# Two layers of a hybrid diffusion backbone: the RWKV branch's preparation and state copy on VectorE instead of GpSimd

## The chip, the core and the metric

The kernel is one program on one core of a Trainium2 chip. The metric is the device time of an execution in microseconds (us). The core has five instruction streams that the profile shows: PE (TensorE's matrix products; PEld is the loading of the stationary operand that runs beside them), DVE (VectorE), ACT (ScalarE), POOL (GpSimd) and SP (SyncE, which here only issues transfers). Each runs its own instructions in a fixed order and waits on semaphores for the others.

## The reference, cut to what matters

One inference step of a two-layer backbone over 384 tokens (128 context, 256 latent) with model width 1024. A layer is a gated feed-forward half step, a mixer, and a second feed-forward half step. The mixer sums three gated branches: windowed attention, neighbourhood attention, and a bidirectional RWKV-7 recurrence with 8 heads of 64 channels, in both directions `d`. Only this last branch is touched:

```
kk = normalised(k * k_k)                        # per head
for d in (forward, backward):
    decay = exp(-exp(-softplus(-(w0[d] + tanh(wlo) @ decay_up[d])) - 0.5))
    a     = sigmoid(a0[d] + alo @ iclr_up[d])
    k_d   = k * (1 + (a - 1) * k_a)
    S     = start state
    for t in tokens of d:
        sa = S @ (-kk_t)
        S  = S * decay_t + outer(sa, kk_t * a_t) + outer(v_t, k_d_t)
        y_t += S @ r_t
    bonus += sum(r * k_d * r_k, per head) * v
out = (group_norm(y) + bonus) * g
```

## The kernel before

**Dense work.** Every large product is 128x128 weights against 128x384 activations, done in three passes with operands split into a high and a low part (`hi`, `lo`); L400 to L402 are the three passes in the mixer. Weights stream from memory in units of eight blocks as `raw`; ACT makes `hi<-raw`, and DVE makes `lo<-raw,hi`.

**The recurrence.** It is computed in chunks of 64 tokens. The eight heads go in four pairs `p` = 0 to 3 (two heads fill 128 partitions), and each pair goes through three generators:

- `rwkv_prepare` makes, for each direction, the running decays `wq` and `wi` (a scan on DVE after an exponential on ACT), the key `kd`, and from them two operands of the chunk algebra: `bk` (half of it `ta` times `wq`, the other half `kd` times `wq`) and `arc` (`r` times `wi` in one half, `nkk` times `wi` in the other). At its end `bo` sums the two directions' `kd` and multiplies by `r` for the bonus; the product `bon` spreads it.
- `rwkv_chunks` transposes `bk` (`pb`), forms the chunks' Gram products (`pg`, masked into `gt` by DVE), inverts a 64x64 triangular system per chunk (block transposes `lu`, short products and reductions in `pr` and `gt`, transposes `yr` and `xt`, four groups of small products called `pz`), and forms `mt`, `rp`, `nt`, `yt`.
- `rwkv_scan` carries the state from chunk to chunk (`sp`, `scan`, `state`), then normalises (`gm`, `gss`) and gates.

**What orders it.** `rwkv_gen` interleaves them: while the chunks of pair `p` run, the scan of pair `p-1` and the preparation of pair `p+1` are advanced a step at a time, and beside them `mixer_fill` supplies the dense products of the gates and of the second branch's projection (`pz`, `pc`, `pp` with L400 to L402). Small constants (`RATES`, `LAT`, `SB`, `SF`, `RA`) set how much dense work is released beside each step. A scheduler then fixes the order of every engine from priorities: chunks stand first (offset `OB` = 200), then scan and weights (100), then preparation (`OA` = 50). What a scheduler takes an instruction to cost enters into that order, so moving an instruction to another engine can move others on all engines.

**Buffers.** `ta`, `wq`, `wi` and `vv` have one buffer, `kd`, `bk` and `arc` two. ACT's exponential into `wi` of the second direction therefore waits until both `arc` halves of the first have been read, and `wq` in the same way for both `bk` halves. GpSimd also zeroes the last column of `wq` and `wi` and copies chunk decays into `pcs`; these stay on it.

A helper records every vector instruction, so the profile shows L290 for all of DVE, ACT and POOL; the tiles' names tell them apart. In the names, `out<-in` is what is written and what is read.

Of the kernel before, what the change touches and what calls it, by code (L numbers as in the profile page):

```python
# [295 lines left out]
def trunk(tc, I, O, order, taps=None, stop=None):  # L296
# [1124 lines left out]
    def rwkv_prepare(l, p, w, pool, x):  # L1421
# [31 lines left out]
        for d in range(2):  # L1453
            ta = pool.tile([P, NTOK], F32, tag="ta", bufs=1, name="ta")
            S.activation(out=ta, in_=rev(pas[d][:, :NTOK], d), func=AF.Tanh, scale=0.5, bias=w["hb"][:, 1, 4 * d + p : 4 * d + p + 1])

            prods = []
            for nm, sc, bc in (("wq", -0.5 * DECAY, "dneg"), ("wi", 0.5 * DECAY, "dpos")):
                t = pool.tile([P, NCH, CH + 1], F32, tag=nm, bufs=1, name=nm)
                G.memset(t[:, :, CH], 0.0)  # L1460
                S.activation(out=t[:, :, :CH], in_=ch(ths[d]), func=AF.Exp, scale=sc, bias=C(bc))
                f = t.rearrange("p c t -> p (c t)")[:, ::-1]
                V.tensor_tensor_scan(f, f, C("one65")[:, ::-1], 0.0, ALU.mult, ALU.add)
                prods.append(t)
            wq, wi = prods
            lat, ctx = (slice(NCC, NCH), slice(0, NCC)) if d == 0 else (slice(0, NCL), slice(NCL, NCH))
            G.tensor_copy(pcs[:, d, 0, 0:NCC], wq[:, ctx, 0])
            G.tensor_copy(pcs[:, d, 1, :], wq[:, lat, 0])
            kd = pool.tile([P, NTOK], F32, tag="kd", bufs=2, name="kd")
            S.activation(out=kd, in_=ta, func=AF.Identity, scale=w["ka"][:, 0, p : p + 1], bias=w["ka"][:, 1, p : p + 1])  # L1470
            G.tensor_tensor(out=kd, in0=kd, in1=rev(k, d), op=ALU.mult)
            kds.append(kd)
            V.scalar_tensor_tensor(out=ta, in0=ta, scalar=1.0, in1=rev(nkk, d), op0=ALU.add, op1=ALU.mult)
            bk = pool.tile([P, NCH, 2, CH], F32, tag="bk", bufs=2, name="bk")
            x["bk"].append(bk)
            V.scalar_tensor_tensor(out=bk[:, :, d, :], in0=ch(ta), scalar=-0.5, in1=wq[:, :, 1:], op0=ALU.mult, op1=ALU.mult)
            G.tensor_tensor(out=bk[:, :, 1 - d, :], in0=ch(kd), in1=wq[:, :, 1:], op=ALU.mult)
            rr, nn = ch(r), ch(nkk)
            if d:
                rr, nn = rr[:, ::-1, ::-1], nn[:, ::-1, ::-1]  # L1480
            G.tensor_tensor(out=arc[:, 0, :, d, :], in0=rr, in1=wi[:, :, 1:], op=ALU.mult)
            V.tensor_tensor(out=arc[:, 1, :, d, :], in0=nn, in1=wi[:, :, :CH], op=ALU.mult)
            yield 1.0

        bo = pool.tile([P, NTOK], F32, tag="ta", bufs=1, name="bo")
        G.tensor_tensor(out=bo, in0=kds[0], in1=kds[1][:, ::-1], op=ALU.add)
        S.activation(out=r, in_=r, func=AF.Copy, scale=vcol(l, "r_k")[:, p : p + 1])
        G.tensor_tensor(out=bo, in0=bo, in1=r, op=ALU.mult)
        pb = rwp("bon")
        rmm(pb[:, :NTOK], C("blk"), bo, start=True, stop=True)  # L1490
        V.tensor_tensor(out=v, in0=v, in1=pb[:, :NTOK], op=ALU.mult)
# [173 lines left out]
    def rwkv_scan(l, p, w, pool, keep, oc, x):  # L1665
# [13 lines left out]
        for j in range(NCL):  # L1679
# [18 lines left out]
            if j < NCL - 1:  # L1698
                nst = pool.tile([P, 2, 2, HD], F32, tag="state", bufs=2, name="state")
                for d in range(2):  # L1700
                    V.tensor_tensor(out=nst[:, d, lo:2], in0=sv[:, d, lo:2], in1=idx_slice(nt[:, d], d, j, lo == 0), op=ALU.add)
                    if j == 0:
                        G.tensor_copy(nst[:, d, 0], nt[:, d, chunk_ids(d, 0)[0], :])
            for d in range(2):
                ys = idx_slice(yt[:, d], d, j, lo == 0)
                V.tensor_tensor(out=ys, in0=yv[:, d, lo:2], in1=ys, op=ALU.add)
# [111 lines left out]
```

## Time and profile before

| | us |
|---|---|
| median of 3 runs | 2420.25 |
| lowest and highest run | 2416.85 and 2423.66 |
| the profiled execution's own time | 2421.42 |
| its span, first to last instruction | 2419.0 |
| PE busy in the span | 2291.4 (95%) |
| DVE busy | 1690.8 (70%) |
| ACT busy | 1058.4 (44%) |
| POOL busy | 408.4 (17%) |

The recurrence lies twice in the span, once per layer, from about 563 to 859 us and from about 1758 to 2054 us; the two runs through it have the same order of instructions and differ little in time. The page's table of 40 slices gives each engine's busy share in time; the windows give the same for chosen stretches. A timeline shows an engine's instructions, and in square brackets how long the engine stood idle before one and what released it.

### The profile page before, as it was taken

The numbers are of one execution on the slowest core, as the hardware profiler recorded it, in microseconds if no ns is written. First come the engines' busy times: TensorE is split into PE (matmuls) and PEld (weight loads), VectorE is DVE, ScalarE is ACT, GpSimd is POOL, SyncE is SP. The second block draws the span as 40 slices with busy tenths as digits, with TensorE's granted clock in tenths as the row PEclk, the third lists the DMA queues.
The fourth block names the chain that finished last, engine by engine and source line by source line (L and its number), as shares of the span: only waits on it lengthen the run. The fifth ranks groups of instructions, "written<-read, shape, count | busy, mean of one in ns | idle before, by whom it ended". The sixth has DMA issues, their size and how long they took to land.

```text
span 2419.0 us, 42727 instructions
## 1 busy us (share of the span) xinstructions
PE 2291.4 (95%) x17066; PEld 2100.0 (87%) x17066; DVE 1690.8 (70%) x2969; ACT 1058.4 (44%) x1942; POOL 408.4 (17%) x426
## 2 busy tenths in 40 slices
PE   8999999998899998999989999899989999999998
PEld 5999988887677788999889999889877777889997
DVE  3797877767767568786978964766687674775534
ACT  3333245655545445333243333555655454443322
POOL 1000421002122143000430003300022120420003
PEclk9999999999999999999999999999999999999998
DMA  8676544241111262665546733523321113534332
GB/s 301 220 242 207 190 121 128 87 118 62 40 58 48 76 216 96 199 217 180 170 148 205 247 131 127 153 80 105 100 71 41 58 50 92 201 106 143 122 127 83
DMA packets 125078, 324.53 MB, mean 134 GB/s; under 512 B 31568, under 2 KB 50256, under 8 KB 124880
## 3 DMA queue, kind: packets, MB, share of 16 engines
q1 hardware_dynamic: 124880, 321.81, 41.2%
q8 instruction: 134, 2.20, 0.4%
q14 instruction: 64, 0.52, 0.1%
HBM read 312.06 MB, written 9.70 MB: 133 GB/s over the span
## 4 chain that ended last, share of the span: by engine, by line
PE 73%; DVE 12%; ACT 5%; issue 4%; POOL 3%; DMA 1%; SPq 0%; POOLq 0%; ACTq 0%; DVEq 0%
PE po L402 5%; PE po L401 5%; PE po L400 5%; PE pg L384 5%; PE pg L385 5%; PE pg L386 5%; PE pa L384 4%; PE pa L385 4%; PE pa L386 4%; DVE lo L290 3%; ACT hi L290 2%; PE pz L400 2%; PE pz L401 2%; PE pz L402 2%; DVE gt L290 1%
## 5 line engine op out<-in xcount | busy, mean ns | idle before, releaser
L290 ACT ACTIVATE hi<-raw 128x1024 fp32r<-128x1024 f32 x418 | 441.7, 1058 | 747.2 <-issue 244.6
L290 DVE TENSOR_TENSOR lo<-raw,hi 128x1024 fp32r<-128x1024 f32 (+1 forms) x472 | 548.3, 1171 | 309.0 <-ACT hi L290 307.6
L290 DVE SCALAR_TENSOR_TENSOR acc<-adaw,cs,acc 128x1024 f32<-128x1024 f32 x224 | 287.8, 1322 | 0.0
L402 PE MATMUL po<-uh,lo 128*128 128x384 f32 x704 | 238.0, 338 | 6.4 <-DVE lo L290 6.4
L400 PE MATMUL po<-uh,hi 128*128 128x384 f32 x704 | 239.5, 340 | 0.0
L401 PE MATMUL po<-ul,hi 128*128 128x384 f32 x704 | 237.7, 338 | 0.0
L384 PE MATMUL pg<-zh,hi 128*128 128x384 f32 x632 | 216.1, 342 | 15.2 <-DVE si L290 9.2
L385 PE MATMUL pg<-zl,hi 128*128 128x384 f32 x632 | 214.9, 340 | 0.0
L386 PE MATMUL pg<-zh,lo 128*128 128x384 f32 x632 | 214.7, 340 | 0.0
L384 PE MATMUL pa<-zh,hi 128*128 128x384 f32 x608 | 206.4, 340 | 0.0
L385 PE MATMUL pa<-zl,hi 128*128 128x384 f32 x608 | 205.2, 337 | 0.0
L386 PE MATMUL pa<-zh,lo 128*128 128x384 f32 x608 | 204.8, 337 | 0.0
L290 POOL TENSOR_TENSOR sa<-ax,ax 128x384 f32<-128x384 f32 x12 | 15.8, 1318 | 809.7 <-DVE ax L290 603.5
L402 PEld LDWEIGHTS po<-uh,lo 128*128 128x128 f32 x704 | 133.3, 189 | 7.4 <-DVE lo L290 7.4
L400 PE MATMUL pz<-zh,hi 128*128 128x384 f32 x352 | 129.1, 367 | 8.4 <-ACT hi L290 5.6
L384 PEld LDWEIGHTS pg<-zh,hi 128*128 128x128 f32 x632 | 120.2, 190 | 18.1 <-ACT hi L290 10.1
L400 PEld LDWEIGHTS po<-uh,hi 128*128 128x128 f32 x704 | 133.3, 189 | 2.2 <-ACT hi L290 0.8
L401 PEld LDWEIGHTS po<-ul,hi 128*128 128x128 f32 x704 | 133.3, 189 | 1.4 <-issue 0.8
L402 PE MATMUL pz<-zh,lo 128*128 128x384 f32 x352 | 126.9, 360 | 3.3 <-DVE lo L290 3.3
L401 PE MATMUL pz<-zl,hi 128*128 128x384 f32 x352 | 124.6, 354 | 0.0
L386 PEld LDWEIGHTS pg<-zh,lo 128*128 128x128 f32 x632 | 120.6, 191 | 1.6 <-issue 1.6
L385 PEld LDWEIGHTS pg<-zl,hi 128*128 128x128 f32 x632 | 120.2, 190 | 0.8 <-issue 0.8
(398 smaller groups left out, 5207.7 us busy)
## 6 DMA issues: line engine op xcount, KB each, us to landing
raw<-ws SPq DMA_DIRECT2D x418, 512.0 KB, 3.5
adaw<-wada SPq DMA_DIRECT2D x144, 512.0 KB, 4.6
bm<-rpb SPq DMA_DIRECT2D x64, 64.0 KB, 6.9
axd<-ax SPq DMA_DIRECT2D x16, 192.0 KB, 5.0
gcd<-gt SPq DMA_DIRECT2D x16, 192.0 KB, 4.6
gc<-gcd SPq DMA_DIRECT2D x16, 192.0 KB, 4.1
ax<-axd SPq DMA_DIRECT2D x16, 192.0 KB, 4.6
xt<-xt SPq DMA_DIRECT2D x8, 192.0 KB, 8.4
```

What stands on the lines that cost most here:

```text
L290: self.last = f(*a, **k)
L384: T.matmul(out, wh, xh, start=first, stop=False)
L385: T.matmul(out, wh, xl, start=False, stop=False)
L386: return T.matmul(out, wl, xh, start=False, stop=last)
L400: T.matmul(out, wh, xh, start=(k == 0), stop=False)
L401: T.matmul(out, wh, xl, start=False, stop=False)
L402: T.matmul(out, wl, xh, start=False, stop=(k == n - 1))
```

## The change

Five operations in `rwkv_prepare` and the copy of one state in `rwkv_scan` are issued to VectorE in place of GpSimd. Operands and results are the same. Per pair that is eight instructions of 128x384 elements (`kd`, one half of `bk` and one half of `arc` for each direction, and two for `bo`) and two copies of 128x64; with four pairs and two layers, 64 and 16.

```
-            G.tensor_tensor(out=kd, in0=kd, in1=rev(k, d), op=ALU.mult)
+            V.tensor_tensor(out=kd, in0=kd, in1=rev(k, d), op=ALU.mult)
...
-            G.tensor_tensor(out=bk[:, :, 1 - d, :], in0=ch(kd), in1=wq[:, :, 1:], op=ALU.mult)
+            V.tensor_tensor(out=bk[:, :, 1 - d, :], in0=ch(kd), in1=wq[:, :, 1:], op=ALU.mult)
...
-            G.tensor_tensor(out=arc[:, 0, :, d, :], in0=rr, in1=wi[:, :, 1:], op=ALU.mult)
+            V.tensor_tensor(out=arc[:, 0, :, d, :], in0=rr, in1=wi[:, :, 1:], op=ALU.mult)
...
-        G.tensor_tensor(out=bo, in0=kds[0], in1=kds[1][:, ::-1], op=ALU.add)
+        V.tensor_tensor(out=bo, in0=kds[0], in1=kds[1][:, ::-1], op=ALU.add)
...
-        G.tensor_tensor(out=bo, in0=bo, in1=r, op=ALU.mult)
+        V.tensor_tensor(out=bo, in0=bo, in1=r, op=ALU.mult)
...
-                        G.tensor_copy(nst[:, d, 0], nt[:, d, chunk_ids(d, 0)[0], :])
+                        V.tensor_copy(nst[:, d, 0], nt[:, d, chunk_ids(d, 0)[0], :])
```

The scheduler's order changes on all engines, but only inside the two recurrences and the few transfers behind them. Three places matter.

**Place 1, pair 0, VectorE.** From the first key to the first masks of the Gram products, before:

```order
L290 SCALAR_TENSOR_TENSOR ta<-ta,nkk 128x384
L290 SCALAR_TENSOR_TENSOR gt<-gt,pp 128x384
L290 SCALAR_TENSOR_TENSOR bk<-ta,wq 128x6x64
L290 SCALAR_TENSOR_TENSOR wq<-wq,con 128x390
L290 TENSOR_TENSOR gt<-pg,con 128x4x128
L290 TENSOR_TENSOR sp<-st_5463,pcs 128x2x64
L290 TENSOR_TENSOR gt<-pg,con 128x2x128
L290 SCALAR_TENSOR_TENSOR ta<-ta,nkk 128x384
```

and after:

```order
L290 TENSOR_TENSOR kd<-kd,k_4043 128x384
L290 SCALAR_TENSOR_TENSOR ta<-ta,nkk 128x384
L290 TENSOR_TENSOR bk<-kd,wq 128x6x64
L290 SCALAR_TENSOR_TENSOR bk<-ta,wq 128x6x64
L290 SCALAR_TENSOR_TENSOR gt<-gt,pp 128x384
L290 TENSOR_TENSOR lo<-raw,hi 128x512 x2
L290 TENSOR_TENSOR gt<-pg,con 128x4x128
L290 TENSOR_TENSOR gt<-pg,con 128x2x128
L290 TENSOR_TENSOR gt<-pg,con 128x4x128
L290 TENSOR_TENSOR gt<-pg,con 128x2x128
L290 SCALAR_TENSOR_TENSOR wq<-wq,con 128x390
L290 TENSOR_TENSOR kd<-kd,k_4043 128x384
```

Both halves of the first `bk` now stand in a row on VectorE, and the scan `wq` of the second direction has moved behind the four masks.

**Place 1, pair 0, TensorE.** The same stretch as a difference (`pz` with L400 to L402 is dense work):

```order
 L401 MATMUL pz<-zl_94,hi 128x384
 L402 MATMUL pz<-zh_93,lo 128x384
+L1350 MATMUL pb<-con,bk 128x128 x6
+L1346 MATMUL pg<-arc,bk 128x128 x4
 L400 MATMUL pz<-zh_95,hi 128x384
 L401 MATMUL pz<-zl_96,hi 128x384
+L1346 MATMUL pg<-arc,bk 128x128 x8
 L402 MATMUL pz<-zh_95,lo 128x384
 L400 MATMUL pz<-zh_97,hi 128x384
 L401 MATMUL pz<-zl_98,hi 128x384
-L1350 MATMUL pb<-con,bk 128x128 x6
-L1346 MATMUL pg<-arc,bk 128x128 x12
```

The transposes of `bk` and the Gram products stand later among the dense products: five later for the first direction. From the last `up` product of pair 0 to its first small `pz` there are 90 dense products now, 84 before.

**Place 2, between pairs 0 and 1, VectorE.** Around the first reads of `pm`, before:

```order
L290 SCALAR_TENSOR_TENSOR wq<-wq,con 128x390
L290 SCALAR_TENSOR_TENSOR wi<-wi,con 128x390
L290 TENSOR_TENSOR mt<-pm,con 128x128
L290 TENSOR_TENSOR rp<-pm,arc 128x128
L290 TENSOR_TENSOR mt<-pm,con 128x256
L290 TENSOR_TENSOR rp<-pm,arc 128x256
```

and after:

```order
L290 SCALAR_TENSOR_TENSOR wi<-wi,con 128x390
L290 TENSOR_TENSOR arc<-r_5387,wi 128x6x64
L290 TENSOR_TENSOR arc<-nkk,wi 128x6x64
L290 TENSOR_TENSOR kd<-kd,k_5307 128x384
L290 SCALAR_TENSOR_TENSOR ta<-ta,nkk 128x384
L290 SCALAR_TENSOR_TENSOR wi<-wi,con 128x390
L290 SCALAR_TENSOR_TENSOR bk<-ta,wq 128x6x64
L290 TENSOR_TENSOR arc<-r_5387,wi 128x6x64
L290 TENSOR_TENSOR arc<-nkk,wi 128x6x64
L290 TENSOR_TENSOR bk<-kd,wq 128x6x64
L290 TENSOR_TENSOR lo<-raw,hi 128x512
L290 TENSOR_TENSOR mt<-pm,con 128x128
```

Nearly the whole preparation of pair 1 has moved in front of `mt`; on ACT both exponentials into `wi` moved ahead of the copies `atq` with it.

**Place 3, pair 2, VectorE.** Ahead of the second group of small products' result `xt<-pz`, before:

```order
L290 SCALAR_TENSOR_TENSOR wi<-wi,con 128x390
L290 TENSOR_TENSOR arc<-nkk,wi 128x6x64
L290 SCALAR_TENSOR_TENSOR gt<-gt,pp 128x384
L290 TENSOR_TENSOR lo<-raw,hi 128x512 x2
L290 SCALAR_TENSOR_TENSOR xt<-pz_7895,con,xt 128x12x16 x2
L290 STREAM_TRANSPOSE yr<-xt 128x384
```

and after:

```order
L290 TENSOR_TENSOR sp<-st_6625,pcs 128x2x64
L290 SCALAR_TENSOR_TENSOR wi<-wi,con 128x390
L290 TENSOR_TENSOR kd<-kd,k_6261 128x384
L290 SCALAR_TENSOR_TENSOR gt<-gt,pp 128x384
L290 SCALAR_TENSOR_TENSOR ta<-ta,nkk 128x384
L290 TENSOR_TENSOR lo<-raw,hi 128x512 x2
L290 SCALAR_TENSOR_TENSOR bk<-ta,wq 128x6x64
L290 TENSOR_TENSOR bk<-kd,wq 128x6x64
L290 SCALAR_TENSOR_TENSOR xt<-pz_7895,con,xt 128x12x16 x2
L290 STREAM_TRANSPOSE yr<-xt 128x384
```

Five instructions of the next pair's preparation now stand in front of it where there were two. TensorE has 9 dense products between the second and third small groups there, where it had 11 and two `up` products.

## Rows read from the trace of the kernel before

**Rows 1.** The page, part 1: busy us (share of span), instructions.

```profile
PE 2291.4 (95%) x17066; PEld 2100.0 (87%) x17066; DVE 1690.8 (70%) x2969; ACT 1058.4 (44%) x1942; POOL 408.4 (17%) x426
```

**Rows 2.** Windows, first layer: length us; PE, PEld, DVE, ACT, POOL busy; clock; DMA.

```profile
563.00:612.00 49.00, 43.29 (x284) 36.95 (x283) 42.63 (x77) 24.40 (x43) 13.07 (x22) 0.99 0.21 66
612.00:660.00 48.00, 42.07 (x691) 33.73 (x691) 32.91 (x72) 25.88 (x52) 10.60 (x18) 0.93 0.12 38
660.00:713.00 53.00, 50.98 (x697) 41.84 (x697) 38.68 (x85) 26.79 (x51) 15.97 (x21) 1.00 0.21 66
713.00:772.00 59.00, 56.38 (x802) 45.71 (x802) 44.91 (x93) 32.48 (x62) 13.99 (x20) 0.97 0.15 49
772.00:859.00 87.00, 80.13 (x1009) 66.63 (x1009) 48.42 (x111) 39.42 (x70) 8.97 (x10) 1.00 0.23 71
```

**Rows 3.** Tile views: count, ns least/median/most, first and last start, forms.

```profile
L290 POOL TENSOR_TENSOR kd<-kd,k x16: 998/1017/1386, 581.2 to 1954.5; 128x384 f32<-128x384 f32 x16
L290 POOL TENSOR_TENSOR bk<-kd,wq x16: 902/1104/1301, 582.7 to 1957.3; 128x384 f32<-128x384 f32 x16
...
L290 POOL TENSOR_TENSOR arc<-r,wi x16: 903/1120/2083, 571.6 to 1942.2; 128x384 f32<-128x384 f32 x16
L290 DVE TENSOR_TENSOR arc<-nkk,wi x16: 521/558/1287, 571.7 to 1942.1; 128x384 f32<-128x384 f32 x16
...
L290 DVE TENSOR_TENSOR state<-scan,nt x48: 176/216/298, 657.8 to 2042.3; 128x64 f32<-128x64 f32 x32, 128x128 f32<-128x128 f32 x16
...
L290 POOL COPY state<-nt x16: 237/238/569, 637.0 to 2036.5; 128x64 f32<-128x64 f32 x16
```

**Rows 4.** Timeline, PE, pair 0: start us, us, instruction, [idle before <-releaser].

```profile
581.09 0.34 PE L400 MATMUL pz<-zh,hi 128*128 128x384 f32 x1
581.26 0.34 PE L401 MATMUL pz<-zl,hi 128*128 128x384 f32 x1
...
583.80 0.87 PE L1350 MATMUL pb<-con,bk 128*128 128x128 f32 x6 [1.34 <-POOL bk L290]
...
590.03 0.85 PE L1350 MATMUL pb<-con,bk 128*128 128x128 f32 x6 [0.37 <-DVE bk L290]
...
612.27 0.98 PE L1346 MATMUL pz<-yr,gt 16*32 16x16 f32 x96 [2.42 <-DVE yr L290]
```

**Rows 5.** Timeline, DVE and POOL, where one holds up the other.

```profile
571.73 1.29 DVE L290 TENSOR_TENSOR arc<-nkk,wi 128x384 f32<-128x384 f32 x1
...
584.79 0.97 DVE L290 TENSOR_TENSOR_SCAN wq<-wq,con 128x390 f32<-128x390 f32 x1 [1.80 <-POOL wq L290]
...
590.14 2.90 DVE L290 TENSOR_TENSOR lo<-raw,hi 128x512 fp32r<-128x512 f32 x2
...
589.96 1.12 POOL L290 TENSOR_TENSOR bo<-kd 128x384 f32<-128x384 f32 x1 [1.89 <-DVE bk L290]
...
762.65 1.30 DVE L290 SCALAR_TENSOR_TENSOR bk<-ta,wq 128x384 f32<-128x384 f32 x1
```

**Rows 6.** Timeline, DVE and PE, between pairs 0 and 1.

```profile
632.77 0.97 DVE L290 TENSOR_TENSOR_SCAN wi<-wi,con 128x390 f32<-128x390 f32 x1 [2.93 <-ACT wi L290]
...
634.27 0.65 PE L1346 MATMUL pm<-gt,atq 64*64 64x128 f32 x8 [0.61 <-DVE rp L290]
...
646.79 0.91 PE L1346 MATMUL bon<-bo,con 128*128 128x384 f32 x2 [1.21 <-POOL bo L290]
```

**Rows 7.** Timeline, DVE and PE, pair 1.

```profile
665.74 2.00 DVE L290 TENSOR_TENSOR lo<-raw,hi 128x512 fp32r<-128x512 f32 x2
...
667.20 0.44 PE L402 MATMUL pz<-zh,lo 128*128 128x384 f32 x1 [1.10 <-DVE lo L290]
```

**Rows 8.** Timeline, DVE and PE, pair 2.

```profile
745.34 1.28 DVE L290 TENSOR_TENSOR lo<-raw,hi 128x512 fp32r<-128x512 f32 x2
...
756.09 0.95 PE L1346 MATMUL pz<-yr,gt 32*32 32x32 f32 x48
```

**Rows 9.** Timeline, PE, pair 3.

```profile
790.55 0.45 PE L1346 MATMUL scan<-sp,mt 64*64 64x64 f32 x8 [1.41 <-DVE v L290]
```

## The prediction

> **What bounds the kernel now.** I read the page's busy times first. TensorE is busy 95% of the span [rows 1], so a change on other engines can gain only what TensorE stands idle, or runs at the lower clock, where they are touched. That place is the recurrence, once in each layer, so I read windows over its first run, one for each pair of heads [rows 2]. TensorE's idle time there is length minus busy: 5.7, 5.9, 2.0, 2.6 and 6.9 us, 23.1 in 296, so about 46 us in both layers: the whole stake of better timing. The second window also has a mean granted clock of 0.93 where the others have 0.97 to 1.00: 48 us times 0.07 is some 3.4 us lost to its lower level, 1.2 GHz, following the pair's longest wait. VectorE is busy 87, 69, 73, 76 and 56% of the five, GpSimd 10 to 30%. So VectorE is the fuller of the two, though not full.
>
> Then I read the tiles [rows 3], to see what each moved instruction costs on either engine, and the waits in TensorE's timeline [rows 4 to 9], to see which of them a moved instruction ends.
>
> **What VectorE takes on, and what it gets back.** GpSimd needs 1.02 to 1.12 us for one 128x384 product [rows 3]. VectorE does the same kind (`arc<-nkk,wi`, same shape, both inputs in SBUF) in 0.56. The copy of 128x64 I take at 0.22, the median of VectorE's addition of that size and its nearest row; it is at most 0.24 on GpSimd. Per layer this is 32 x 0.56 + 8 x 0.22 = 19.7 us on VectorE, from about 37 us on GpSimd.
>
> But GpSimd's instructions cost VectorE time while they run. Two `lo<-raw,hi` took 2.90 us beside the two `bo` instructions [rows 5], against 1.28 elsewhere [rows 8]. I compared every VectorE instruction that overlaps a moved one with its own form elsewhere: 20 in a layer are longer by over 0.1 us, from `arc<-nkk,wi` with 1.29 against 0.56 to `bk<-ta,wq` with 1.30 against about 0.55 [rows 5], 11.6 us in all. So VectorE's net load grows by 19.7 - 11.6 = 8.1 us a layer, from 208 to 216 of 296.
>
> The Trainium skill (SBUF — State Buffer, Who interferes with whom) says that a VectorE instruction with two SBUF inputs and a GpSimd instruction that reads SBUF exclude each other for the whole instruction. The trace agrees where both are ready, as with `lo` and `bo`. Were every moved instruction to block VectorE for its whole length, 37 us a layer would come back, not 11.6; the overlap that the trace has is what counts.
>
> **Where TensorE waits: the sum for one layer.** Dense products follow each other every 0.17 us [rows 4], and this converts moved products into time.
>
> *Pair 0.* TensorE stood 1.34 us for GpSimd's half of `bk`, and 2.42 us for `yr` [rows 4]. Now `kd`, `ta` and both halves of `bk` are four VectorE instructions, 2.2 us from ACT's `kd`, where GpSimd's two took up to 1.39 + 1.10 [rows 3]; and five more dense products (0.87 us) stand in front of the wait, so it closes. Up to `yr` VectorE gets eight instructions (4.5 us) and three parts of a convolution that stood later (1.3), and loses 4.4 of the 11.6 us and up to 1.8 us of idling behind GpSimd's queue [rows 5]: `yr` comes within -0.4 to +1.4, I take +0.2. TensorE has six dense products and three small transposes more before it: 1.4 us. Idle time changes by 0.2 - 1.4 = **-1.2** (-1.8 to 0).
>
> *Between pairs 0 and 1.* TensorE waited 0.61 us for `rp`, since VectorE had idled 2.93 us for ACT's `wi` and then run its scan, 0.97, ahead of `mt` and `rp`; and 1.21 us for `bo` [rows 6]. The exponential now comes earlier on ACT, and `bo` is two instructions of 0.56 in place of about 1.1. If both waits go, -1.8. Against it: eight instructions, a scan and one `lo`, 6.1 us, stand in front of `mt`, of which 2.9 us fill the old idle time and about 2.7 stood behind `mt` before; the rest and a late ACT could give +1.0. I take **-1.6**, near the waits' rows.
>
> *Pair 1.* One dense product waited 1.10 us for `lo` [rows 7], which took 2.00 us beside GpSimd's `arc` of 2.08 us [rows 3], not 1.28: -0.7; but the new `arc` stands in front of it, +0.6. **-0.1** (-1.1 to +0.6).
>
> *Pair 2.* Ahead of `xt<-pz` VectorE now has a scan (0.97), four 128x384 products and a gate's (five times 0.56) and two `lo` (1.28): 5.1 us. TensorE has nine dense products, 1.6 us, and four scan products between the second and third small groups; before, it did not wait there [rows 8]. If TensorE arrives as early as the queue starts, it waits some 3 us; if VectorE has run ahead, nothing. I take **+2.0** (0 to +3.1). This is the price of the change.
>
> *Pair 3* has no preparation beside it. A scan's wait of 1.41 us [rows 9] goes, since that scan stands earlier. TensorE comes to the first small group 19 dense products earlier (3.3 us), and VectorE's queue loses two updates of `v` and two `lo`, 2.4 us: +0.9 - 1.4 = **-0.5** (-1.4 to +0.9).
>
> The state copies stand where `nt` is waited for anyway, and cost nothing while the additions behind them wait for the same tile; without that cover they cost 0.2 us each, 1.8 a layer, already in VectorE's load. GpSimd's remaining zeroings and `pcs` copies no longer queue behind products, in my -0.4 for pair 0. Behind the recurrence the dense remainder covers the last gating as before.
>
> Sum: -1.2 - 1.6 - 0.1 + 2.0 - 0.5 = -1.4 us a layer, -2.8 in both. Against the profiled execution's own 2421.42 (its span of 2419.0 and 2.4 around it) that is 2418.6; that execution lies 1.2 above the median, 2420.25, so I forecast **2417.4** for the median. A measurement of this kernel can tell a change of about 0.3%, 7.3 us: the forecast lies within.
>
> **The rivals.**
>
> *The waits collapse and the clock with them* (faster). All low ends hold but pair 2's price is half: -1.8 - 1.8 - 1.1 + 1.0 - 1.4 = -5.1 a layer; 3.4 us more if the shorter wait for `yr` leaves the clock up. Without the clock 2410, with it 2403; I set 2408. For it: the waits named end on GpSimd or on what GpSimd delayed. Against: the second window's idle time is spread over many short waits.
>
> *VectorE becomes the bound* (slower). The inversions of pairs 1 and 2 are chains on VectorE into which the next pair's preparation is now cut. If TensorE has run out of dense work there, VectorE's net 8.1 us lie on the path, less the 2.55 us that TensorE waited for GpSimd [rows 4, 6]: +5.5 a layer, +11: 2431. It decides at `xt<-pz` of pair 2: from a wait of about 3 us on, the gain is eaten. For it: 76% busy over the window and no slack inside the chain. Against: GpSimd's interference goes. The Trainium skill (Perfetto Trace Analysis, Optimizing Scalar/DVE Operations) speaks against this change: with VectorE saturated, work may be worth moving to ScalarE or even GpSimd; it adds that the two share a read port. By that rule this rival's time would come; at 69 to 87% the windows show it close to full, not full.
>
> *Nothing moves* (hidden). TensorE's order is filled anyway and the waits only change places: 2420.
>
> **How the numbers follow.** Forecast 0.40 (2413 to 2422), collapse 0.24, VectorE bound 0.21, hidden 0.15. Faster by over 0.3%, under 2413.0: 0.22 of the collapse and 0.06 of the forecast's edge, 0.28. Slower, over 2427.5: 0.18 of VectorE's bound and 0.03 of the forecast, 0.21. Within: 0.51. For eight in ten the range must hold most of both rivals: 2406 to 2431. All low ends of the terms together give -6.1 a layer, 2408 (2401 with the clock), all high ends +5.6, 2431.
>
> **What the profile will show.** Right: GpSimd's busy time near 335 us; VectorE's near 1707; `arc<-nkk,wi` never far over 0.56; no wait of `pb` or `bon` for GpSimd; the wait for `yr` in pair 0 about 1 us shorter; a new wait of 1 to 3 us behind `xt<-pz` in pair 2. Wrong: a VectorE total up by the full 39 us (no interference given back), or TensorE's idle time in the recurrence moving by more than 4 us a layer, or a different count of stretches at the lower clock.

## The result, and the profile after

The changed kernel takes **2435.92 us** (median of 7 runs, 2428.36 to 2438.17); the kernel before, timed beside it, 2423.66 (7 runs, 2416.85 to 2426.72). The ratio is 1.0056, with a 95% interval of 1.0042 to 1.0070: slower by some 13 us, outside the forecast's range. The profiled execution of the changed kernel is the fastest of its seven, 2428.36 us with a span of 2426.6, so what follows shows a little less than the whole loss.

Part 1 of its page, to be laid beside [rows 1]: busy us (share of span), instructions.

```profile
PE 2306.6 (95%) x17066; PEld 2112.7 (87%) x17066; DVE 1691.8 (70%) x3049; ACT 1061.7 (44%) x1946; POOL 327.6 (14%) x346
```

TensorE runs the same 17066 instructions, and is busy 15.2 us longer with them (2306.6 - 2291.4). Its idle time, span less busy, **fell**: 120.0 us, where before it was 127.6. So -7.6 of idle and +15.2 of busy make the +7.6 between the two spans. VectorE took 80 instructions more for 1.0 us more of busy time. No engine's load explains a slower kernel; TensorE taking longer over the same instructions does.

Where, the windows tell, the same five as in [rows 2] (length us; PE, PEld, DVE, ACT, POOL busy; granted clock; DMA). A clock of 1.00 means 2.4 GHz over the whole stretch, 0.50 means 1.2 GHz.

```profile
563.00:612.00 49.00, 42.93 (x378) 37.22 (x376) 42.79 (x87) 25.56 (x45) 4.15 (x11) 0.97 0.27 84
612.00:660.00 48.00, 47.11 (x527) 35.74 (x524) 27.14 (x58) 22.47 (x44) 2.08 (x9) 0.75 0.05 16
660.00:713.00 53.00, 50.69 (x758) 42.36 (x758) 43.82 (x107) 30.19 (x56) 4.19 (x10) 1.00 0.22 68
713.00:772.00 59.00, 54.69 (x735) 44.69 (x731) 46.75 (x102) 33.34 (x62) 6.86 (x12) 0.91 0.15 48
772.00:859.00 87.00, 81.88 (x1052) 67.26 (x1050) 44.83 (x112) 34.03 (x64) 5.46 (x5) 0.94 0.19 60
```

Idle time (length less PE) is 6.1, 0.9, 2.3, 4.3 and 5.1 us, 18.7 in all where before it was 23.1. But the clock column reads 0.97, **0.75**, 1.00, 0.91, 0.94 where before it read 0.99, 0.93, 1.00, 0.97, 1.00. In the second window TensorE hardly waits, 0.9 us of 48, and spends half of it at the lower level, 1.2 GHz: 48 x 0.25 x 2 = 24 us. In the second layer the same window (1807 to 1855) has 0.89 after and 0.93 before. Over both recurrences, before:

```profile
563.00:859.00 296.00, 272.86 (x3480) 224.86 (x3479) 207.56 (x435) 148.98 (x277) 62.60 (x91) 0.98 0.19 60
1758.00:2054.00 296.00, 273.70 (x3488) 225.48 (x3485) 207.56 (x435) 149.10 (x277) 62.77 (x92) 0.98 0.19 60
```

and after:

```profile
563.00:859.00 296.00, 277.31 (x3432) 227.28 (x3431) 205.33 (x464) 145.58 (x269) 22.74 (x47) 0.92 0.18 56
1758.00:2054.00 296.00, 274.71 (x3466) 225.31 (x3464) 210.61 (x479) 150.33 (x282) 23.35 (x50) 0.95 0.18 58
```

That is about 77 us at the lower level where there were 24. The two second windows make some 21 of these 53 us more, and pair 3's, which go from 1.00 to 0.94 in both layers, another 21.

What stands there, TensorE's timeline (start us, us, instruction, [idle before <-releaser]):

```profile
605.01 0.49 PE L1350 MATMUL spread<-con,rb 128*128 128x128 f32 x3
610.56 1.47 PE L1346 MATMUL pz<-yr,gt 16*32 16x16 f32 x96 [5.06 <-DVE yr L290]
...
617.55 0.52 PE L400 MATMUL pc<-zh,hi 128*128 128x384 f32 x1
617.87 0.52 PE L401 MATMUL pc<-zl,hi 128*128 128x384 f32 x1
...
619.60 1.65 PE L1346 MATMUL up<-tw,wl 64*128 64x384 f32 x2
621.17 1.49 PE L1346 MATMUL pz<-yr,gt 32*32 32x32 f32 x48
```

Before, TensorE stood 1.34 and 0.37 us for `bk` and 2.42 for `yr`, with smaller waits for masks between [rows 4]. Now the early waits are gone, TensorE is through its dense products sooner, and stands once, 5.06 us, for `yr`. Behind that wait dense products follow each other every 0.32 us (617.55, 617.87) instead of every 0.17 [rows 4], the first small group takes 1.47 us instead of 0.98, and `up` (half-size products of the next pair's preparation), which before stood behind the small groups, now stands between them.

The moved instructions on VectorE, tile views as in [rows 3] (count, ns least/median/most, first and last start, forms):

```profile
L290 DVE TENSOR_TENSOR kd<-kd,k x16: 528/548/561, 577.8 to 1959.5; 128x384 f32<-128x384 f32 x16
...
L290 DVE TENSOR_TENSOR bk<-kd,wq x16: 544/548/552, 578.7 to 1960.4; 128x384 f32<-128x384 f32 x16
...
L290 DVE TENSOR_TENSOR arc<-nkk,wi x16: 547/550/559, 569.6 to 1962.6; 128x384 f32<-128x384 f32 x16
...
L290 DVE COPY state<-nt x16: 181/195/196, 644.0 to 2044.4; 128x64 f32<-128x64 f32 x16
```

They cost what was forecast, 64 x 0.55 + 16 x 0.195 = 38 us in both layers, and VectorE got back 37 of them: `arc<-nkk,wi` has no instruction over 0.56 us any more.

### The profile page after: what moved, and what is told of

Its sections match the earlier page's. It is cut to its first block, busy times and chain, and to the rows that moved or that the text cites. A ratio compares the mean times of both kernels' runs of the same rounds, so it can differ in the third digit from the quotient of the medians.

```text
span 2426.6 us, 42703 instructions
## 1 busy us (share of the span) xinstructions
PE 2306.6 (95%) x17066; PEld 2112.7 (87%) x17066; DVE 1691.8 (70%) x3049; ACT 1061.7 (44%) x1946; POOL 327.6 (14%) x346
## 4 chain that ended last, share of the span: by engine, by line
PE 72%; DVE 11%; issue 8%; ACT 4%; POOL 2%; DMA 0%; POOLq 0%; ACTq 0%; DVEq 0%
PE po L402 5%; PE po L401 5%; PE po L400 5%; PE pg L384 5%; PE pg L385 5%; PE pg L386 5%; PE pa L384 4%; PE pa L385 4%; PE pa L386 4%; DVE lo L290 2%; PE pc L400 1%; PE pz L400 1%; PE pg L1346 1%; ACT hi L290 1%; PE pz L402 1%
## 5 line engine op out<-in xcount | busy, mean ns | idle before, releaser
L290 DVE TENSOR_TENSOR lo<-raw,hi 128x1024 fp32r<-128x1024 f32 (+1 forms) x472 | 537.7, 1147 | 318.9 <-ACT hi L290 316.5
L402 PE MATMUL po<-uh,lo 128*128 128x384 f32 x704 | 238.0, 338 | 6.4 <-DVE lo L290 6.4
L400 PE MATMUL po<-uh,hi 128*128 128x384 f32 x704 | 239.5, 340 | 0.0
L402 PEld LDWEIGHTS po<-uh,lo 128*128 128x128 f32 x704 | 133.3, 189 | 7.4 <-DVE lo L290 7.4
L400 PE MATMUL pz<-zh,hi 128*128 128x384 f32 x352 | 132.8, 378 | 4.8 <-ACT hi L290 4.8
L400 PEld LDWEIGHTS po<-uh,hi 128*128 128x128 f32 x704 | 133.3, 189 | 2.2 <-ACT hi L290 0.8
L402 PE MATMUL pz<-zh,lo 128*128 128x384 f32 x352 | 127.1, 362 | 1.8 <-DVE lo L290 1.6
```

Source lines behind the costliest of these rows:

```text
L290: self.last = f(*a, **k)
L400: T.matmul(out, wh, xh, start=(k == 0), stop=False)
L402: T.matmul(out, wl, xh, start=False, stop=(k == n - 1))
```

## The experiments

Theory A: the new order of the queues lets TensorE's clock fall for longer. Theory B: VectorE's longer queue is itself the cost. Each kernel ran beside the kernel before on the same chip; three chips served in all, and the kernel before had medians of 2421 to 2424 us and a mean granted clock of 0.983 to 0.984 on them. The clock here is the mean over a kernel's timed runs.

| kernel | six operations on | order of the queues, and edit | median us | ratio, 95% interval | clock |
|---|---|---|---|---|---|
| changed kernel | VectorE | new | 2435.9 | 1.0056 (1.0042 to 1.0070) | 0.972 |
| g_new_order | GpSimd | new | 2437.8 | 1.0058 (1.0042 to 1.0073) | 0.972 |
| v_old_order | VectorE | old | 2439.7 | 1.0067 (1.0053 to 1.0080) | 0.977 |
| before_rate | GpSimd | another | 2441.4 | 1.0075 (1.0057 to 1.0092) | 0.976 |
| after_rate | VectorE | another | 2447.8 | 1.0100 (1.0083 to 1.0117) | 0.970 |
| after_front | VectorE | another | 2436.2 | 1.0054 (1.0037 to 1.0071) | 0.977 |
| after_filled | VectorE | new, wait for yr filled | 2430.0 | 1.0023 (1.0009 to 1.0038) | 0.977 |
| before_filled | GpSimd | old, wait for yr filled | 2423.9 | 0.9999 (0.9985 to 1.0013) | 0.985 |
| after_between | VectorE | new, 4 x 10 added behind it | 2429.1 | 1.0030 (1.0019 to 1.0041) | 0.980 |
| after_between5 | VectorE | new, 4 x 5 added behind it | 2434.6 | 1.0043 (1.0027 to 1.0059) | 0.976 |
| before_between | GpSimd | old, 4 x 10 added | 2430.5 | 1.0030 (1.0017 to 1.0043) | 0.985 |
| old_arc | arc on VectorE | old | 2431.6 | 1.0033 (1.0019 to 1.0048) | 0.980 |
| old_kdbk | kd, bk on VectorE | old | 2430.0 | 1.0028 (1.0015 to 1.0042) | 0.982 |
| old_bo | bo on VectorE | old | 2423.4 | 1.0000 (0.9988 to 1.0013) | 0.983 |
| after_up_first | VectorE | new, two up moved ahead | 2429.4 | 1.0022 (1.0009 to 1.0035) | 0.973 |
| up_first_between5 | VectorE | the same, 4 x 5 added | 2425.5 | 1.0009 (0.9994 to 1.0023) | 0.979 |
| best | VectorE | the same, waits filled too | 2414.9 | 0.9964 (0.9953 to 0.9975) | 0.983 |
| best_g | GpSimd | as best | 2420.7 | 0.9993 (0.9981 to 1.0006) | 0.981 |
| best_waits | VectorE | two up ahead, only waits filled | **2407.7** | 0.9932 (0.9912 to 0.9952) | 0.983 |

### Engine or order

Both come with one edit, since the scheduler orders by what it takes an instruction to cost. To part them, an order is written down as a list of instructions for each engine, and each instruction is made to be issued behind the one ahead of it in the list; the moved ones alone stay where the scheduler puts them. Writing an order down costs nothing by itself: old_bo and before_filled, which have the old order in this form, take 2423.4 and 2423.9 us.

```
+    for row in rows:
+        for x, y in zip(row, row[1:]):
+            tc.add_manual_dep(by[f"I-{y}"], f"I-{x}", mybir.DependencyInfo(mybir.DependencyClass.NoSync, mybir.DependencyReason.DATA), reason="pinned")
```

**g_new_order**: GpSimd's code, the changed kernel's order.

> The converse: the six operations on GpSimd as before, but every engine issues all other instructions in the order of the changed kernel. Theory A: TensorE's idle time is gathered in front of yr in pair 0 here too, with a low-clock stretch of more than 10 us behind it, and the time is 2430 us or more. Theory B: VectorE's queue is short again, so about 2420 us.

It is as slow as the changed kernel, and its second window looks the same:

```profile
612.00:660.00 48.00, 46.37 (x613) 35.60 (x614) 26.24 (x49) 22.44 (x44) 12.14 (x19) 0.74 0.08 26
```

Clock 0.74, with GpSimd doing the old work (12.1 us). So VectorE's load is not needed for the loss: the new order alone makes one of this size, as theory A expected. VectorE is busy 1683.2 us on its page, 7.6 less than before with the same instructions, which the new order alone gives back. With the new order held, the move to VectorE thus adds 8.6 us to it (1691.8 - 1683.2), not 1.0.

**v_old_order**: the changed code, the order before.

> The changed kernel's engines (the six operations on VectorE), but every engine issues all other instructions in the order of the kernel before; the moved ones stand where the scheduler puts them between those. It separates the engine from the order. Theory A (the order and the waits it makes let TensorE's clock fall): the wait for yr in pair 0 is split again as before (about 2.4 us or less, not 5.06), the low-clock stretch behind it is short (3 to 10 us, not 27), and the time is that of before or a little under: 2412 to 2424 us. Theory B (VectorE's longer queue is itself the cost): as slow as the changed kernel, 2430 us or more.

Of theory A's forecast the wait alone came true: 2.43 us for `yr` again. The low stretch behind it is 10 us in the first layer and 14 in the second (6.8 before), the second windows read 0.82 and 0.79, and the time is 2439.7, not 2412 to 2424: in theory B's range. So the old order doesn't save it: it fits GpSimd. Its page:

```profile
PE 2307.8 (95%) x17066; PEld 2114.2 (87%) x17066; DVE 1700.0 (70%) x3049; ACT 1058.4 (43%) x1942; POOL 332.6 (14%) x346
```

The span is 2435.6 us, so idle time is 127.8 us where it was 127.6 before, and nearly all of the 16.6 us between the spans is TensorE's busy time, 16.4 more. Where a new wait comes from can still be seen. ACT's timeline between pairs 0 and 1 shows one, in v_old_order:

```profile
637.05 0.62 ACT L290 ACTIVATE wi<-th,con 128x384 f32<-128x384 f32 x1 [2.19 <-DVE arc L290]
```

and in the kernel before:

```profile
637.61 0.62 ACT L290 ACTIVATE wi<-th,con 128x384 f32<-128x384 f32 x1 [0.93 <-POOL state L290]
```

GpSimd had made `arc` beside VectorE's `mt` and `rp`; in one queue it stands behind them, behind `kd`, a state copy that waits for `nt`, `ta` and `bk`. ACT's exponential waits for it, `yt` stands behind that, and TensorE 1.80 us for `yt` where it had been 0.59:

```profile
638.10 0.66 PE L1350 MATMUL pb<-con,bk 128*128 128x128 f32 x4 [1.80 <-ACT yt L290]
```

Other waits shrank by as much, since the idle time is that of before. The mean clock is 0.977 here: a longer VectorE queue in an order that doesn't fit it, too, leaves TensorE longer at the lower level. Taken together, the order alone costs 14 to 15 us, the engine alone 16, and both 12: the two don't add up.

**before_rate**: no engine changed, one constant, which reorders pairs 1 to 3.

```
-RATES = (0.4, 0.2, 0.8, 0.3)
+RATES = (0.4, 0.2, 1.2, 0.3)
```

> The control: the kernel before (GpSimd) with RATES[2] = 1.2 in place of 0.8, which changes the order and no engine. Between the small groups it leaves 3, 7, 6 dense products in pair 0, 0, 7, 5 in pair 1 (37, 31, 8 before), 4, 11, 0 in pair 2 and 1, 12, 19 in pair 3. Theory A1: few dense products between the groups, so more low clock than in the kernel before and 8 to 20 us slower, 2431 to 2444 us, with no engine changed. Theory B: near 2424 us.

Slower by 20 us (2441.4 against 2421.4), as theory A expected, with nothing but the order changed: more than the whole loss in question. On its page busy time has 12.0 us of this (2303.4) and idle time 10.1 (137.7, span 2441.1), so here the clock is only a part.

### The wait, and what stands behind it

The added products read two resident tiles and write a buffer that the next small group writes over; nothing reads their results.

```
+    def idle(out, p, n):
+        for _ in range(0 if p else n):
+            T.matmul(out[:, :NTOK], hs[0][0][:, :P], hs[1][0], start=True, stop=True)
...
         pz = atp("pz2")
+        idle(pz, p, 10)
```

**after_filled** (28 in the wait) and **before_filled** (14):

> The changed kernel with 28 products of 128x384 added on TensorE right in front of the first small products of pair 0, in each layer; nothing reads their results, and all else keeps its order. By the 0.17 us of a dense product they take 4.8 us, nearly the 5.06 us for which TensorE stands idle there for yr. Theory A: the idle time closes, the 27.3 us at the lower clock behind it shrink to less than 7, and the time falls by 8 to 14 us, to 2422 to 2428. Theory B: the wait is VectorE's, filling it changes nothing: 2434 to 2438, more if the added products run over.

> The kernel before with 14 such products (2.4 us) in the same place, where TensorE waits 2.42 us for yr. Theory A: the stretches of 6.8 us at the lower clock behind that wait, one in each layer, go, which is worth up to 3.4 us each: 2416 to 2421 us. Theory B: no change from 2423.7, or up to 3 us slower where the products run over.

The changed kernel gains 6 us, between what the two theories gave, and the kernel before nothing, as theory B had it. The low stretch did not go: the second window of after_filled still reads 0.79 in both layers.

```profile
612.00:660.00 48.00, 46.23 (x620) 35.12 (x618) 28.40 (x60) 23.45 (x46) 2.08 (x9) 0.79 0.08 26
1758.00:1807.00 49.00, 46.46 (x295) 39.16 (x296) 37.52 (x82) 23.89 (x45) 4.74 (x14) 0.93 0.23 76
1807.00:1855.00 48.00, 46.67 (x612) 36.59 (x610) 30.35 (x66) 23.42 (x45) 1.57 (x8) 0.79 0.12 38
```

And the wait itself is filled there:

```profile
607.61 5.10 PE L1582 MATMUL pz<-zh,zh 128*128 128x384 f32 x28
613.03 0.99 PE L1346 MATMUL pz<-yr,gt 16*32 16x16 f32 x96 [0.32 <-DVE yr L290]
```

TensorE stands 0.32 us for `yr`, the clock holds over the first small group, and then falls all the same: a window from 616.8 to 637.3 reads 0.50, with 20.0 of 20.5 us busy. So this wait isn't needed for the low stretch. The next kernels leave it and add products behind it.

**after_between** (10 in front of each of four groups), **after_between5** (5) and the control **before_between** (10):

> The changed kernel with 10 products of 128x384 added in front of the second, third and fourth groups of small products of pair 0 and of the products p behind them, 40 in each layer; nothing reads their results, and all else keeps its order. The wait for yr of about 5 us is left as it is. By 0.174 us each they are 7.0 us of work a layer, 13.9 in both. Theory A1 (what stands behind the wait keeps the clock low: small products and the half-size products up with few dense ones between): the low-clock stretch of pair 0 ends early, under 11 us in both layers where the changed kernel has 27.3 and 10.2, and the time rises by less than the added work, to 2438 to 2446 us. Theory A2 (the wait itself sets the length): the stretch stays at 10 to 27 us, the added products run in part at the lower clock, and the time is 2450 us or more.

> The changed kernel with 5 instead of 10 products in front of each of the four groups, 20 in each layer, 7.0 us in all; nothing reads their results. Theory A1: if they are enough for the clock, the low stretch of pair 0 is again about 10 us and the time some 7 us under that with ten, 2421 to 2427 us; if they are too few, the stretch is 14 to 27 us and the time 2428 to 2436.

> The control for the 40 added products a layer between pair 0's small groups: the same edit in the kernel before, whose stretch at the lower clock there is 6.8 us in each layer. Theory A1: there is little clock to win (at most 6.8 us at half rate, 3 us a layer) against 13.9 us of added work, so it is slower than the kernel before: 2429 to 2436 us. If it came out faster than before, or as fast, the added products would do something else than hold the clock.

In after_between TensorE has 13.9 us of unneeded work more than the changed kernel, and the time is 6.8 us **less**. The window shows why: clock 0.91 instead of 0.75 (0.89 in the second layer, as in the changed kernel).

```profile
612.00:660.00 48.00, 46.30 (x652) 37.97 (x653) 27.65 (x59) 22.46 (x45) 2.08 (x9) 0.91 0.09 26
```

Its page has TensorE's busy time with 80 products more:

```profile
PE 2308.7 (95%) x17146; PEld 2117.2 (87%) x17146; DVE 1693.0 (70%) x3049; ACT 1062.0 (44%) x1946; POOL 325.7 (13%) x346
```

Less their 13.9 us that is 2294.8: of the 15.2 us that the same instructions took longer in the changed kernel, 11.8 are gone. The same products in the kernel before, which had little clock to win, cost 6.7 us, as expected. Half as many are too few: 2434.6, with 13.6 us at the lower level in one layer and 34 in the other. That added work can pay shows the clock at work in the changed kernel's loss; the gain was larger than theory A had put it (2438 to 2446).

**after_rate** and **after_front**: VectorE's code in two other orders of the scheduler's own (RATES as above; `OA = 150` for 50).

> The changed kernel with one constant changed: RATES[2], the rate at which dense products are released beside the small groups, 1.2 in place of 0.8. The scheduler then puts 31, 39 and 13 dense products between the small groups of pair 2 (0, 9 and 5 in the changed kernel; 4, 31 and 4 before), pair 0 stays as it is. Theory A1: the low-clock stretches of pair 2 go, that of pair 0 stays; 2425 to 2432 us. Theory B (VectorE's longer queue is the cost): 2433 us or more.

> The changed kernel with the priority of the preparation raised: OA = 150 in place of 50, so that the next pair's preparation stands earlier in all queues. The dense products between the small groups are 3, 16 and 5 in pair 0, 46, 33 and 7 in pair 1, 7, 20 and 8 in pair 2, 18, 8 and 12 in pair 3. Theory A1: more dense products between the groups of pairs 2 and 3 than in the changed kernel, so less low clock; 2424 to 2434 us. Theory B: the preparation cuts further into the inversions on VectorE, so slower than the changed kernel, 2438 us or more.

Both missed what theory A gave: 2447.8 and 2436.2. By the time alone after_rate lies where theory B put it. It spread dense products between pair 2's groups, as meant, and its page shows what came of it:

```profile
PE 2338.8 (95%) x17066; PEld 2134.0 (87%) x17066; DVE 1691.4 (69%) x3049; ACT 1062.9 (43%) x1946; POOL 336.8 (14%) x346
```

TensorE's idle time is 113.5 us (span 2452.3), less than in either kernel, and it is busy 47 us longer than before with the same instructions, at a mean clock of 0.968. Idle time and total time go opposite ways here. The lower clock can account for at most 40 of these 47 us (0.032 of 2452 us lost to it, against 0.016 of 2419 before); the rest wasn't traced. Dense products between one pair's groups didn't raise the clock of the whole: pair 2's window went from 0.91 to 0.94 only, the second one is at 0.72 and pair 3's at 0.93.

### Which of the moved operations costs in the old order

One part moved at a time, all else in the old order; the edits are the diff's own lines.

> Only r times wi (arc) moved to VectorE, all other instructions of every engine in the order of the kernel before. Where all six were moved in that order, ACT's exponential into wi stood 2.19 us for VectorE's arc between pairs 0 and 1 (0.93 us for GpSimd before). If arc itself is the cause (its place behind mt and rp in VectorE's queue), this wait is again about 2 us or more, and the time 2430 to 2438 us. If it is what stands ahead of arc there (kd, a state copy and bk), the wait is near 1 us and the time that of the kernel before, 2419 to 2426.

> Only the keys (kd and its half of bk) moved to VectorE, in the old order: 16 instructions of 0.56 us a layer, standing between masks of the Gram products and products of the inversion. If VectorE's queue between pairs 0 and 1 and in the chains is the cause of the 16 us, most of it appears here: 2428 to 2438 us. If the parts only hurt together, 2421 to 2427.

> Only the two bonus instructions (bo) moved to VectorE, in the old order. They hold up VectorE's lo for 1.6 us on GpSimd (2.90 against 1.28 us) and TensorE waited 1.21 us for the second bo between pairs 0 and 1; both should go. By theory A they cost nothing in the chains: 2418 to 2425 us. If VectorE's load counts as such, 2426 or more.

`bo` costs nothing, as expected, `arc` 8 us, the keys 6, which is not the most of it that their first case asked for; together 14 of the 16 us. The state copy wasn't moved by itself. old_arc fits neither of its two cases: ACT waits 0.66 us for `arc`, so the wait that v_old_order shows seems to come from what stands ahead of `arc` there, not from `arc` itself; yet it is slower. TensorE's wait for `yr` is 2.40 us, as before, and what differs is the clock behind it:

```profile
612.14 0.99 PE L1346 MATMUL pz<-yr,gt 16*32 16x16 f32 x96 [2.40 <-DVE yr L290]
```

```profile
612.00:660.00 48.00, 44.01 (x670) 35.00 (x670) 27.61 (x54) 24.95 (x50) 8.11 (x16) 0.79 0.08 27
```

This profile is of old_arc's slowest run, 2439 us. Its idle time is 127.7 us (span 2437.3, busy 2309.6), again that of before. Equal waits, then, are followed by unequal stretches at the lower level.

### A version faster than both

**after_up_first** puts real work into the wait: two of the `up` products stand in front of the first small group, with VectorE's reads of `bon` and `spread` ahead of `yr`, so that their buffers are free.

```
+L1346 MATMUL up<-tw,wl 128x384 x2
 L1346 MATMUL pz1<-yr,gt 32x16 x48
...
-L1346 MATMUL up<-tw,wl 128x384
```

**up_first_between5** adds 5 products before each group to it; **best** fills the waits besides (16 ahead of `up`, 12 in pair 3's first wait); **best_g** is best with GpSimd's code; **best_waits** is best without the 20 between the groups.

> The changed kernel with the first two up products of pair 1 (the half-size products that stand between pair 0's small groups and keep TensorE from dense work there) moved in front of the first small group, into the wait for yr; so that they find their buffers free, VectorE's reads of bon and spread stand ahead of yr and two lo behind it, and ACT's tanh of the first up right behind the first small group. Nothing is added. Theory A1: the wait for yr falls from 5.06 to some 3.3 us, the stretch at the lower clock in pair 0 is at most 10 to 14 us in both layers, and the time falls by 4 to 10 us, to 2426 to 2432. Theory A2 (only dense products in between raise the clock, the up products don't matter): low clock of pair 0 stays at 20 us or more in one layer, and the gain is under 3 us.

> Both edits together: two up products in the wait for yr and 5 added products in front of each of the four groups. Theory A1: the low stretch of pair 0 is 7 us or less in both layers, and the time is that of the kernel before or less, 2416 to 2425 us, with all six operations on VectorE and 7.0 us of work that nothing reads. Theory B (VectorE's queue is the cost): it can't come under 2430 us.

> All six on VectorE, the order of the changed kernel with two up products moved ahead (as in after_up_first), and unused products of 128x384 in TensorE's waits and between pair 0's small groups: 16 in the wait ahead of up, 5 in front of each of the four groups, 12 in pair 3's first wait, 48 in a layer; the 28 in waits take idle time, the 20 between add 3.5 us a layer. Theory A: the low-clock stretches of pairs 0 and 3 get shorter still, 2416 to 2424 us. Theory B: not under 2428 us.

> The fast version's order and its 48 added products a layer, with the six operations on GpSimd as in the kernel before. If the engine matters little where the order fits (2437.8 against 2435.9 us in the changed kernel's order), 2414 to 2420 us. If the move to VectorE carries the gain, 2422 us or more, with TensorE's waits for bk and bo back between pairs 0 and 1.

> The fast version without the 20 added products between pair 0's small groups, so only the 28 in a layer that stand in TensorE's waits. That takes 7.0 us of work away. If dense products between the small groups are what keeps the clock up, the low stretch of pair 0 is back at 10 to 24 us in each layer (3.4 in the fast version) and the time is 2415 to 2424 us, no better than with them; if filling the waits is enough, the stretch stays under 7 us and the time falls to 2406 to 2412.

after_up_first gains 6.5 us, as theory A1 had it, but not by the clock: the mean is 0.973, and the stretch is 23.9 us in both layers, which was theory A2's sign. TensorE does not wait at all in it:

```profile
611.60:635.50 23.90, 23.90 (x359) 18.21 (x360) 14.44 (x28) 11.61 (x23) 0.63 (x5) 0.50 0.09 29
```

Its profiled execution is only 0.6 us under the changed kernel's, with 3.0 us less idle and 2.4 us more busy time, so where the 6.5 us come from stays open. up_first_between5 takes 2425.5 us, just over its forecast, with 13.6 us at the lower level in both layers and not 7 or less; it is under the 2430 that theory B allowed. best is 8.7 us under the kernel before, with all six operations on VectorE. In its order GpSimd's code takes 5.8 us more, between its two cases, and the two intervals don't meet: in this order the move to VectorE is a gain. No order was fitted to GpSimd's code in the same way, so the 8.7 us are not the worth of the move. And best_waits is faster still, by just the 7 us of work that it leaves out. It is 16 us under the kernel before and 28 under the changed one. Its page and timeline:

```profile
PE 2299.4 (96%) x17122; PEld 2109.5 (88%) x17122; DVE 1691.8 (70%) x3049; ACT 1062.1 (44%) x1946; POOL 330.3 (14%) x346
```

```profile
605.91 3.02 PE L1498 MATMUL pz<-zh,zh 128*128 128x384 f32 x16
609.23 1.37 PE L1347 MATMUL up<-tw,wl 64*128 64x384 f32 x4 [0.29 <-DVE v L291]
611.26 0.99 PE L1347 MATMUL pz<-yr,gt 16*32 16x16 f32 x96 [0.66 <-DVE yr L291]
```

Of 5.06 us of waiting 0.95 are left. TensorE's idle time is 104.0 us (span 2403.4), 23.6 under the kernel before; 56 products of 0.174 us take 9.7 of these, and the clock, 0.983, is that of before. So 23.6 - 9.7 = 13.9 of the 15.6 us between the spans is idle time that went. GpSimd's code was not run in this order. The low stretch of pair 0 is short in the first layer (0.93 in its window) and long in the second (0.90 and 0.89), so the time fell as the second case said, and the clock did so in one layer of two.

## Why the prediction was wrong, point by point

- **VectorE's load.** Forecast +16 us in both layers (19.7 - 11.6 each), measured +1.0. The added 38 us were right; what comes back was 37 us, not 23. With the order held it is about 30: VectorE's busy time rises by 8.6 us from g_new_order to the changed kernel and by 9.2 from the kernel before to v_old_order. The other 8 came with the new order. I had counted only instructions that were longer than their like by over 0.1 us. Had every moved instruction blocked VectorE for its whole length, the prediction's 37 us a layer would have given 74 back. The Trainium skill (SBUF — State Buffer, Who interferes with whom) says that a VectorE instruction with two SBUF inputs and a GpSimd instruction that reads SBUF exclude each other. It doesn't say how often they meet; here some 30 of the 74 us came back with the order held.
- **Idle time, pair 0** (-1.2). The waits for `bk` and the masks closed, as forecast, but what they freed came back nearly whole in front of `yr`. In the first two windows together 11.6 us became 7.0, most of it from the next point. "The wait for `yr` about 1 us shorter" failed: it grew by 2.6 us. I let TensorE's work count against that wait, but not the waits ahead of it that fell away.
- **Between pairs 0 and 1** (-1.6). Right: the waits of 0.61 for `rp` and 1.21 for `bo` [rows 6] are gone. The window's idle time fell by 5.0, though, more than these waits; that TensorE at the lower clock filled the rest with the same work is likely, not shown.
- **Pair 1** (-0.1). The window's idle time went from 2.0 to 2.3 us.
- **Pair 2** (+2.0). The size was right, 2.6 to 4.3 us, the place wrong: there is no wait behind `xt<-pz` for the third group; the time went into waits of 1.01, 1.06 and 1.13 us for `gp`, `lo` and within the second group.
- **Pair 3** (-0.5). Its scan's wait [rows 9] went, others of 2.28 and 1.66 us at the first two groups came: 6.9 to 5.1 us in the window.
- **The sum** (-1.4 a layer). Measured in the windows -4.4 in the first layer, and -1.0 in the second (22.3 to 21.3 of 296). The sign held; the size was luck in part, for the terms missed both ways (+0.4 us in the first window, -5.0 in the second), and the first layer moved by more than the 4 us that the prediction gave as a sign of being wrong.
- **The step that failed.** The sum prices idle time alone and takes TensorE's own work as fixed: "Dense products follow each other every 0.17 us [rows 4], and this converts moved products into time". In the low stretch they follow every 0.32 us, and the same 17066 instructions took 15.2 us longer. The clock came in only as something to win (3.4 us, in the first rival) and in "a different count of stretches" as a sign of error; in the sum it was put at nothing. It cost more than all terms together: 0.983 to 0.972. What that is worth can be estimated within one kernel, whose instructions don't change from run to run: in after_filled 2419.2 us at 0.983 and 2439.0 at 0.973. A line through all runs, each kernel's about its own mean, gives about 1.5 us for 0.001 (single kernels 0.05 to 2.7), and so do the two profiled executions, 15.2 us of busy time for 0.010. So 0.011 is some 17 us; less 7.6 of idle time, about +9 of the 12 to 14 measured.
- **The rivals.** "VectorE becomes the bound" named nearly the right time, 2431, for the wrong reason: the place at which it should decide has no wait, VectorE's load grew by 1.0 us, and GpSimd's code in the same order is as slow. "The waits collapse and the clock with them" had the right quantity with the wrong sign.

What stays open: what makes the clock fall, and what sets how long TensorE stays at the lower level. In after_filled it fell without the long wait. The same order gives 0.75 in one layer and 0.89 in the other (changed kernel), and old_arc's wait is the one of before with another clock behind it. And of the 16.4 us that TensorE is busy longer in v_old_order, the clock of its profile (0.984 to 0.976, by 1.5 us for 0.001 some 12) leaves 4 that weren't traced.

## What to carry to other kernels

Moving an instruction to another engine under a scheduler is two changes, and the second, the order, can weigh as much as the first: hold the order fixed, and change it alone, before the engine is judged. VectorE was worse in the old order, by 16 us, no different clear of noise in the new one (2435.9 against 2437.8), and better by 5.8 in best's. Where TensorE is busy 95% of the time, read its busy time for the same instructions and its granted clock beside its idle time: here less idle time went with more time. Short waits that are closed can come back as one long wait further on. Filling such a wait with work, useful or not, cost nothing in the kernel before and gained 6 us in the changed one.

## What the runs showed of the hardware

- In the changed kernel the granted clock fell to 1.2 GHz during a wait of 5.06 us, and TensorE stayed there from 608.7 to 636.0, busy 25.4 of these 27.3 us; what it ran were groups of 16 to 32 rows and columns, half-size `up` products and 19 dense ones. The Trainium skill (TensorE: Matmul & The Clock Gate, Why this matters for your kernels) warns of idle gaps between bursts of products. The changed kernel's trace agrees for the fall; after_filled's does not, where the wait was 0.32 us and the clock fell for 20.5 us all the same, in both layers.
- A stretch without any wait can stay slow: in after_up_first TensorE was busy 23.9 of 23.9 us at 0.50.
- 80 products that nothing reads made a kernel 6.8 us faster (after_between), and cost 6.7 us where the clock was up (before_between).
- Two VectorE instructions of the same kind took 0.55 us each in place of one on GpSimd of 1.1 us beside one on VectorE of up to 1.29 [rows 3, 5]: GpSimd's busy time fell by 80.8 us (408.4 to 327.6), VectorE did that work in 38 and got 37 back, about 30 of them with the order held.
